# A decoder block on one core: both DRAM writes of a turning ahead of its reads, users six steps on, delayed tasks anchored

## The chip, the cores and the metric

The kernel runs on one core of one Trainium2 chip, as one program. The metric is the device time of one execution in microseconds (us). Engines are PE (matmul), ACT, DVE and POOL (all with queues of their own), and SP, which here only issues DMAs.

## What is computed

One layer of a transformer block on 256 tokens with a width of 2048, in float32. Cut to what matters:

```python
h = h + 0.5 * swiglu(rms_norm(h), ffn1)              # gate, up 2048x5632, down 5632x2048
n = rms_norm(h); P = n @ w_in                        # retention q k v g, window q k v
ret = gate * group_norm(retention(rope(rq), rope(rk), rv))      # 8 heads of 128
swa = sliding_window_attention(rope(sq), rope(sk), sv, sinks)   # 16 heads of 64
h = h + concat(ret, swa) @ w_out
h = h + cross_attention(rms_norm(h), rms_norm(mem))  # 4 heads of 512 into 256 rows
h = h + 0.5 * swiglu(rms_norm(h), ffn2)
out = rms_norm(h)
```

Every one of the products with weights reads its weights from HBM once, 1 MB at a time.

## The kernel before

**Products.** The matrix of each product with weights is cut into units: one unit makes a 256 x 512 piece of an output, `acc`, in two halves of 128 tokens. A step takes 256 rows of the weights (half a MB), so a unit over the depth of 2048 has eight. Weights and activations are each split in a high and a low part of 32 bits, and `three` (L432 to L436) issues high by high (L434), high by low (L435) and low by high (L436). With two slices of 128 rows and two token halves a step is 12 matmuls of 128x128 by 128x512.

**Weights.** `load` and `load_pair` issue 1 MB on SP into `wf` (3 buffers), and `split` makes two steps' parts of it: ACT copies the high part, `wh` (L70), and DVE subtracts for the low part, `wl` (L75). There are 4 buffers of each, and `prepare` splits LOOKAHEAD = 3 steps ahead.

**Turnings.** A result has tokens on its partitions, and its user often needs it the other way round. `cross` (L409) turns two halves of 128x512. DVE transposes blocks of 32x32 (L417) into `sq`, POOL issues a DMA to a DRAM tile `box` (L419, 256 KB) and four DMAs back (L422, 64 KB each) into `dst`, and then the second half goes the same way. POOL issues in order, so the second half's write stands behind the reads of the first, and those wait until the first write has landed. All users of a turning are called by `then`, TURN = 4 steps later. Five functions turn: residual adds (`to_h`, add at L445), the gated FFN blocks (`ffn`, `made`), the retention's q and k (`rqk_done`, `finish` with L690 to L696), the cross attention's keys and queries (`put_done`), and `turn_h`, which brings h back to tokens on partitions in FFN2.

**Behind a residual add** stand the next norm's copies of h (`gained`, L70 on ACT and L329 on DVE), the squares (L362 on ACT), their sum (L366 on DVE) and, two steps after the last, `finish`, whose matmul with ones (L377) gives the mean of squares. The retention scores (`ret_scores`, L705) stand behind `finish` of `rqk_done`. The memory's norm is made in w_out's stage too: `mem_block` loads `mem` on SP (L782) into t2k tiles.

**What sets the order.** `run_stream` writes the steps out in order. Between two steps it runs the tasks that are due: `later(n, f)` sets a task n steps ahead. A scheduler then reorders the instructions of each engine as their dependences and its own times allow; the calls of `pin` fix the order of the first 16 steps as written, and all of SP's. Working tiles come from pools: `t2k` (128x512) has 10 buffers, `blk` 13; `acc` has 2, so a unit's accumulator has to be read by ACT (SILU at L470, scaled copies) or DVE (L477) before the unit two further starts.

**The start** interleaves the first gate and up unit. `prepare` splits one step ahead there.

Of the kernel before, what the change touches and what calls it, by code (L numbers as in the profile page):

```python
# [30 lines left out]
TAIL = 4  # L31
WARM = 9
FIRST = 16
TURN = 4
SWA_EVERY = 5


# [1 line left out]
def decoder_block(ctx: ExitStack, tc: tile.TileContext, a: dict, out: bass.AP):  # L39
# [67 lines left out]
    def when(ready, delay, fn):  # L107
# [5 lines left out]
                later(1, attempt)  # L113
        later(delay, attempt)

    def run_due():
        while True:
            due = [x for x in tasks if x[0] <= clock[0]]
            if not due:
                return  # L120
            x = min(due, key=lambda x: (x[0], x[1]))
            tasks.remove(x)
            x[2]()

    def run_until(ready):
        while not ready():
            x = min(tasks, key=lambda x: (x[0], x[1]))
            tasks.remove(x)
            x[2]()

    class Unit:

# [64 lines left out]
    def pin(engines=None):  # L197

        prev = {}
        for ins in nc.cur_bb.bb.instructions:  # L200
            if engines is not None and ins.engine not in engines:
                continue
            if ins.engine in prev:
                tc.add_manual_dep(
                    ins, prev[ins.engine].name,
                    mybir.DependencyInfo(mybir.DependencyClass.NoSync, mybir.DependencyReason.DATA),
                    reason="program order",
                )
            prev[ins.engine] = ins

    def run_stream():
# [48 lines left out]
        held = []  # L260
        for at, (u, b, ks, _, first, last) in enumerate(steps):
            if at < FIRST:
                prepare(at + 1)
                run_due()
                prepare(at + 2)
            else:
                run_due()
                if at == FIRST:
                    pin()
                prepare(at + 1 + LOOKAHEAD)  # L270
            run_until(lambda: b in u.lhs)
            x = u.lhs[b]
            if first:
                u.acc = [ps_acc.tile([P, 2, 512], F32, tag="acc", name=nm("acc"))] * 2
                if u.per_half:
                    u.acc[1] = ps_acc.tile([P, 2, 512], F32, tag="acc", name=nm("acc"))
            wh, wl = ready.pop(at)
            if at == 0:
                for i, k in enumerate(ks):
                    for t in range(2):  # L280
                        by_tokens(u, u.acc[t], x, wh[:, i : i + 1, :], wl[:, i : i + 1, :], [k], t, first and i == 0, False)
            else:
                for t in range(2):
                    y = (u, u.acc[t], x, wh, wl, ks, t, first, last)
                    if u.per_half and t == 1 and at >= len(steps) - TAIL:
                        held.append(y)
                    else:
                        by_tokens(*y)
            clock[0] += 1
            if last:  # L290
                if u.per_half:
                    u.done(u.acc[0], 0)
                    for y in held:
                        by_tokens(*y)
                    u.done(u.acc[1], 1)
                else:
                    u.done(u.acc[0])
# [106 lines left out]
            nc.vector.tensor_tensor(x, x, r, ALU.mult)  # L404

    def squares_of(x):
        return x.rearrange("p (q g j) -> p q g j", q=4, g=4)

    def cross(src, then, delay=TURN):  # L409

        out = []
        for v in src:
            sq, dst = t2k(), t2k()
            nc.vector.transpose(sq.rearrange("p (g q j) -> p q g j", g=4, q=4), v)  # L417
            box = dram.tile([P, 512], F32, tag="box", name=nm("box"))
            nc.gpsimd.dma_start(box, sq)  # L419
            far = box.rearrange("(i r) (g n) -> g r i n", i=4, g=4)  # L420
            for g in range(4):
                nc.gpsimd.dma_start(dst[32 * g : 32 * g + 32, :].rearrange("p (i n) -> p i n", i=4), far[g])  # L422
            out.append(dst.rearrange("p (i q j) -> p q i j", i=4, q=4))
        later(delay, lambda: then(out))

# [13 lines left out]
    def to_h(w, lhs, factor, blocks, norm=None, then=None):  # L439

        def done(acc, b):
            def add(out):
                for t in range(2):
                    v = hT[b][:, :, t * P : (t + 1) * P].rearrange("p q (a j) -> p q a j", a=4)
                    nc.vector.tensor_tensor(v, v, out[t], ALU.add)  # L445
# [5 lines left out]
            s = [acc[:, t, :] for t in range(2)]  # L451
            if factor != 1.0:
                for t in range(2):
                    s[t] = t2k()
                    copy(s[t], acc[:, t, :], scale=factor)
            cross([squares_of(x) for x in s], add)
        for b in range(4):
            Unit(w, b, 512, lhs, lambda acc, b=b: done(acc, b), blocks, pair=True)

    def ffn(norm, w_gate, w_up, down):  # L460
# [12 lines left out]
        def up_done(b):  # L473
            def done(acc):
# [201 lines left out]
    def rqk_done(g, which):  # L676
        def done(acc):
            def finish(out):
# [21 lines left out]
            cross([squares_of(acc[:, t, :]) for t in range(2)], finish)  # L700
        return done

    def ret_scores(g, i, qk):
# [9 lines left out]
    def rv_done(g):  # L713
        def done(acc):
# [3 lines left out]
            def half(t):  # L718
# [19 lines left out]
                for i in range(4):  # L738
# [70 lines left out]
    def v_done(i):  # L809
# [233 lines left out]
```

## Time and profile before

| what | value |
|---|---|
| median of 3 runs | 2288.42 us (2285.37 to 2296.56) |
| the profiled execution | 2288.49 us |
| its span (first to last instruction) | 2286.7 us |
| PE busy, share of the span | 2203.9 us, 96% |
| DVE, ACT, POOL busy | 1290.5, 1023.8, 309.0 us |
| mean clock granted to PE | 0.982 |
| DMA, mean over the span | 206 GB/s |

A line of a timeline holds start and length of an instruction in us, the engine, the line of the program, the operation with its tiles (buffer numbers left out), and in brackets the engine's idle time ahead of it and the instruction that released it. A released wait ends with the last of its conditions. PEclk is the granted share of PE's full clock.

### The profile page before, as it was taken

How to read it: one execution, taken by the hardware profiler on the slowest of the kernel's cores; microseconds unless marked ns; L12 is line 12 of the kernel's file. 1: busy time of each engine (PE TensorE's matmuls, PEld its weight loads, DVE VectorE, ACT ScalarE, POOL GpSimd, SP SyncE). 2: the span in 40 equal slices, each digit the busy share in tenths (PEclk: the TensorE clock that was granted, in tenths of full speed). 3: DMA queues.
4: the chain of work that ended last, by engine and by line, in shares of the span. 5: the costliest groups of instructions: out<-in, count | busy, mean ns of one | idle time of the engine just before them, and what ended most of it. 6: DMA issues, size and time to landing. Idle time of an engine off the chain costs nothing.

```text
span 2286.7 us, 25822 instructions
## 1 busy us (share of the span) xinstructions
PE 2203.9 (96%) x9868; PEld 1821.7 (80%) x9868; DVE 1290.5 (56%) x1532; ACT 1023.8 (45%) x1257; POOL 309.0 (14%) x557
## 2 busy tenths in 40 slices
PE   9999999999999999989699999999899999999998
PEld 7788888888878888877488878887688888878886
DVE  5655555555556688775455655575455554545554
ACT  5444444444445454544344544454344443444443
POOL 0110111110111101111122001132300100010100
PEclk9999999999999999999799999999899999999999
DMA  6666666666566545545466655476666655566663
GB/s 240 234 208 225 216 225 226 214 215 231 206 224 228 192 167 182 185 148 202 164 212 234 215 187 184 171 251 215 228 205 209 226 198 194 200 205 221 208 221 142
DMA packets 132732, 472.05 MB, mean 206 GB/s; under 512 B 15616, under 2 KB 16384, under 8 KB 132480
## 3 DMA queue, kind: packets, MB, share of 16 engines
q1 hardware_dynamic: 109856, 413.57, 51.7%
q0 software_dynamic: 22464, 56.66, 7.9%
q8 instruction: 77, 1.26, 0.2%
q14 instruction: 47, 0.39, 0.0%
q10 hardware_dynamic: 288, 0.18, 0.0%
HBM read 439.93 MB, written 30.41 MB: 206 GB/s over the span
## 4 chain that ended last, share of the span: by engine, by line
PE 41%; DMA 5%; issue 3%; POOL 2%; ACT 1%; DVE 1%; ACTq 0%; POOLq 0%; DVEq 0%
PE acc L435 13%; PE acc L436 13%; PE acc L434 13%; DMA t2k<-box 3%; DMA box<-t2k 2%; POOL t2k L422 2%; ACT wh L70 1%; DVE wl L75 0%; ACT blk L70 0%; PE tmp L436 0%; PE tmp L377 0%; PE tmp L434 0%; PE tmp L435 0%; DVE t2k L366 0%; ACT t2k L70 0%
## 5 line engine op out<-in xcount | busy, mean ns | idle before, releaser
L75 DVE TENSOR_TENSOR wl<-wf,wh 128x1024 fp32r<-128x1024 f32 (+1 forms) x773 | 938.1, 1221 | 688.1 <-ACT wh L70 687.2
L434 PE MATMUL acc<-wh,blk 128*128 128x512 f32 (+1 forms) x3104 | 1215.4, 392 | 34.4 <-ACT wh L70 22.1
L435 PE MATMUL acc<-wl,blk 128*128 128x512 f32 (+1 forms) x3104 | 1213.8, 391 | 8.9 <-DVE wl L75 8.9
L436 PE MATMUL acc<-wh,blk 128*128 128x512 f32 (+1 forms) x3104 | 1211.9, 390 | 0.0
L70 ACT ACTIVATE wh<-wf 128x1024 fp32r<-128x1024 f32 (+1 forms) x773 | 811.6, 1058 | 888.9 <-PE acc L436 859.4
L434 PEld LDWEIGHTS acc<-wh,blk 128*128 128x128 f32 x3104 | 587.3, 189 | 158.0 <-ACT wh L70 24.7
L435 PEld LDWEIGHTS acc<-wl,blk 128*128 128x128 f32 x3104 | 587.3, 189 | 133.1 <-DVE wl L75 13.6
L436 PEld LDWEIGHTS acc<-wh,blk 128*128 128x128 f32 x3104 | 587.4, 189 | 121.4 <-DVE blk L75 0.4
L422 POOL DMA_DIRECT2D t2k<-box x432 | 235.8, 553 | 397.6 <-DMA box<-t2k 222.3
L419 POOL DMA_DIRECT2D box<-t2k x108 | 61.2, 567 | 1343.7 <-DVE t2k L417 1341.3
L70 ACT ACTIVATE blk<-t2k 128x512 fp32r<-128x512 f32 (+2 forms) x74 | 46.1, 623 | 194.7 <-DMA t2k<-box 192.8
L75 DVE TENSOR_TENSOR blk<-t2k,blk 128x512 fp32r<-128x512 f32 (+1 forms) x66 | 44.7, 678 | 131.7 <-ACT blk L70 131.5
L445 DVE TENSOR_TENSOR h<-h,t2k 128x512 f32<-128x512 f32 x32 | 22.1, 691 | 70.8 <-DMA t2k<-box 70.8
L417 DVE STREAM_TRANSPOSE t2k<-t2k 128x512 f32<-128x512 f32 x76 | 53.6, 705 | 13.4 <-ACT t2k L70 13.4
L70 ACT ACTIVATE blk<-h,gains 128x256 fp32r<-128x256 f32 x64 | 27.6, 498 | 20.5 <-DVE h L445 18.6
L477 DVE SCALAR_TENSOR_TENSOR t2k<-acc,n,t2k 128x512 f32<-128x512 f32 x44 | 31.0, 746 | 7.6 <-PE acc L436 7.6
L470 ACT ACTIVATE t2k<-acc,n 128x512 f32<-128x512 f32 x44 | 27.7, 682 | 16.8 <-PE acc L436 16.7
L70 ACT ACTIVATE blk<-tmp 128x512 fp32r<-128x512 f32 (+2 forms) x49 | 21.5, 450 | 26.3 <-DVE blk L75 12.8
L329 DVE SCALAR_TENSOR_TENSOR blk<-h,gains,blk 128x256 fp32r<-128x256 f32 x64 | 27.0, 480 | 2.4 <-ACT blk L70 2.4
L362 ACT ACTIVATE t2k<-h 128x512 f32<-128x512 f32 x32 | 18.2, 618 | 19.2 <-DVE h L445 19.2
L366 DVE TENSOR_TENSOR t2k<-t2k,t2k 128x512 f32<-128x512 f32 x35 | 23.8, 685 | 3.4 <-ACT t2k L362 1.8
L377 PE MATMUL tmp<-ones,t2k 128*128 128x1 f32 x40 | 6.8, 291 | 15.4 <-DVE t2k L366 15.4
(125 smaller groups left out, 519.4 us busy)
## 6 DMA issues: line engine op xcount, KB each, us to landing
wf<-in_ffn_w_down SPq DMA_DIRECT2D x88, 1024.0 KB, 4.9
wf<-in_ffn_w_gate SPq DMA_DIRECT2D x87, 1024.0 KB, 5.1
wf<-in_ffn_w_up SPq DMA_DIRECT2D x87, 1024.0 KB, 5.4
box<-t2k POOLq DMA_DIRECT2D x108, 256.0 KB, 3.4
t2k<-box POOLq DMA_DIRECT2D x432, 64.0 KB, 3.5
wf<-in_w_in_rqk SPq DMA_DIRECT2D x16, 1024.0 KB, 5.0
wf<-in_w_in_rvg SPq DMA_DIRECT2D x16, 1024.0 KB, 5.1
wf<-in_w_out SPq DMA_DIRECT2D x16, 1024.0 KB, 5.8
```

The lines of the kernel that those rows point to most:

```text
L70: return nc.scalar.activation(dst, src, AF.Copy, **kw)
L75: nc.vector.tensor_tensor(lo, src, hi, ALU.subtract)
L329: nc.vector.scalar_tensor_tensor(x[:, k, 1, :], v[:, k, :], g, x[:, k, 0, :], ALU.mult, ALU.subtract)
L366: nc.vector.tensor_tensor(self.sums, self.sums, y, ALU.add)
L417: nc.vector.transpose(sq.rearrange("p (g q j) -> p q g j", g=4, q=4), v)
L419: nc.gpsimd.dma_start(box, sq)
L422: nc.gpsimd.dma_start(dst[32 * g : 32 * g + 32, :].rearrange("p (i n) -> p i n", i=4), far[g])
L434: nc.tensor.matmul(o, ah, bh, start=start, stop=False)
L435: nc.tensor.matmul(o, ah, bl, start=False, stop=False)
L436: nc.tensor.matmul(o, al, bh, start=False, stop=stop)
L470: nc.scalar.activation(gated[b][t], acc[:, t, :], AF.Silu, scale=norm.scale(t))
L477: nc.vector.scalar_tensor_tensor(s[t], acc[:, t, :], norm.scale(t), s[t], ALU.mult, ALU.mult)
```

## The change

It changes four things.

1. `cross` issues both transposes and both writes first, and then the eight reads. Where the source is a working tile (`room`) the reads land in that tile, and no third tile is taken for a half.
2. TURN is 6 rather than 4. `put_done` asks for 5 steps, and calls `attend` at once instead of one step later. The group norm's halves go from 2 and 3 steps to 4 and 5.
3. `run` executes a delayed task and then ties each of its PE, ACT and DVE instructions behind the last instruction that was written for that engine before the task; the scheduler can't put them ahead of it.
4. At the start, steps 1 to 3 have their weights split in halves, step 1's ahead of two of the norm's copies, and from step 8 the splits run four steps ahead.

```diff
-TURN = 4
+TURN = 6
...
+    def run(x):
+        tasks.remove(x)
+        last = look()
+        at = seen[0]
+        x[2]()
+        for ins in nc.cur_bb.bb.instructions[at:]:
+            if ins.engine in anchored and ins.engine in last:
+                order(last[ins.engine], ins)
...
-                    ready[at] = split(loaded[at], steps[at][0].n, 1)
+                    ready[at] = split(loaded[at], steps[at][0].n, 2 if at < 4 else 1)
...
-                prepare(at + 1)
+                prepare(at + 2 if at == 0 else at + 1)
                 run_due()
-                prepare(at + 2)
+                prepare(at + 2 if at < 8 else at + 1 + LOOKAHEAD)
...
-    def cross(src, then, delay=TURN):
+    def cross(src, then, room=None, delay=TURN):
-        out = []
-        for v in src:
-            sq, dst = t2k(), t2k()
-            nc.vector.transpose(sq.rearrange("p (g q j) -> p q g j", g=4, q=4), v)
+        out, boxes = [], []
+        for i, v in enumerate(src):
+            sq = t2k()
+            nc.vector.transpose(sq.rearrange("p (g q j) -> p q g j", g=4, q=4), squares_of(v))
             box = dram.tile([P, 512], F32, tag="box", name=nm("box"))
             nc.gpsimd.dma_start(box, sq)
-            far = box.rearrange("(i r) (g n) -> g r i n", i=4, g=4)
+            boxes.append(box.rearrange("(i r) (g n) -> g r i n", i=4, g=4))
+        for i, box in enumerate(boxes):
+            dst = t2k() if room is None else room[i]
             for g in range(4):
-                nc.gpsimd.dma_start(dst[...].rearrange("p (i n) -> p i n", i=4), far[g])
+                nc.gpsimd.dma_start(dst[...].rearrange("p (i n) -> p i n", i=4), box[g])
...
-                cross([squares_of(x) for x in s], made)
+                cross(s, made, s)
...
-            later(2, lambda: half(1))
-            later(3, lambda: half(0))
+            later(4, lambda: half(1))
+            later(5, lambda: half(0))
...
                 if then is not None:
-                    later(1, then)
-            cross([squares_of(x) for x in s], made)
+                    then()
+            cross(s, made, s, TURN - 1)
```

Three places in the order of instructions. The first is DVE at the first residual add after FFN1's down product. The names in the rows are of tiles: `wl` low parts of weights, `wf` the loaded weights, `t2k` the turned halves, `h0` the first block of h. Before:

```order
L75 TENSOR_TENSOR wl_766_4612<-wf_764_4609,wh_765_4611 128x1024
L417 STREAM_TRANSPOSE t2k_769_4631<-t2k_767_4627 128x4x4x32
L75 TENSOR_TENSOR wl_776_4650<-wf_764_4609,wh_775_4649 128x1024
L75 TENSOR_TENSOR wl_780_4669<-wf_778_4666,wh_779_4668 128x1024
L417 STREAM_TRANSPOSE t2k_772_4640<-t2k_768_4629 128x4x4x32
L75 TENSOR_TENSOR wl_782_4685<-wf_778_4666,wh_781_4684 128x1024
L445 TENSOR_TENSOR h0_75<-h0_75,t2k_770_4632 128x4x128
L75 TENSOR_TENSOR wl_785_4703<-wf_783_4700,wh_784_4702 128x1024
L75 TENSOR_TENSOR wl_791_4737<-wf_783_4700,wh_790_4736 128x1024
L445 TENSOR_TENSOR h0_75<-h0_75,t2k_773_4641 128x4x128
```

and after (L437 is the transpose, L467 the add):

```order
L75 TENSOR_TENSOR wl_736_4588<-wf_734_4585,wh_735_4587 128x1024
L437 STREAM_TRANSPOSE t2k_739_4607<-t2k_737_4603 128x4x4x32
L437 STREAM_TRANSPOSE t2k_741_4611<-t2k_738_4604 128x4x4x32
L75 TENSOR_TENSOR wl_744_4624<-wf_734_4585,wh_743_4623 128x1024
L75 TENSOR_TENSOR wl_748_4643<-wf_746_4640,wh_747_4642 128x1024
L75 TENSOR_TENSOR wl_750_4659<-wf_746_4640,wh_749_4658 128x1024
L75 TENSOR_TENSOR wl_753_4677<-wf_751_4674,wh_752_4676 128x1024
L75 TENSOR_TENSOR wl_755_4693<-wf_751_4674,wh_754_4692 128x1024
L75 TENSOR_TENSOR wl_758_4711<-wf_756_4708,wh_757_4710 128x1024
L467 TENSOR_TENSOR h0_75<-h0_75,t2k_737_4603 128x4x128
L467 TENSOR_TENSOR h0_75<-h0_75,t2k_738_4604 128x4x128
L75 TENSOR_TENSOR wl_764_4745<-wf_756_4708,wh_763_4744 128x1024
```

The two transposes had two weight splits between them and now stand side by side, and both adds stand together, six weight splits behind the second transpose, where they stood one and three behind it.

The second place is ACT in w_out's stage, from the second of two `wh` of one load. L362 (after: L382) are squares, and `blk` the norms' copies of `mem`. Before:

```order
L70 ACTIVATE wh_1425_8111<-wf_1413_8061 128x1024
L362 ACTIVATE t2k_1423_8106<-t2k_1406_8023 128x512
L362 ACTIVATE t2k_1424_8108<-t2k_1407_8024 128x512
L70 ACTIVATE blk_1438_8184<-t2k_1428_8128,gains_79 128x256 x2
L70 ACTIVATE blk_1438_8184<-t2k_1429_8129,gains_79 128x256 x2
L362 ACTIVATE t2k_1439_8193<-t2k_1428_8128 128x512
L362 ACTIVATE t2k_1440_8196<-t2k_1429_8129 128x512
L362 ACTIVATE t2k_1441_8201<-h1_76 128x512
L362 ACTIVATE t2k_1442_8204<-h1_76 128x512
L70 ACTIVATE wh_1431_8134<-wf_1430_8132 128x1024
L70 ACTIVATE wh_1433_8150<-wf_1430_8132 128x1024
L70 ACTIVATE wh_1436_8168<-wf_1435_8166 128x1024
```

and after:

```order
L70 ACTIVATE wh_1384_8065<-wf_1375_8029 128x1024
L70 ACTIVATE wh_1388_8084<-wf_1387_8082 128x1024
L70 ACTIVATE blk_1390_8100<-t2k_1373_8025,gains_79 128x256 x2
L70 ACTIVATE blk_1390_8100<-t2k_1374_8026,gains_79 128x256 x2
L382 ACTIVATE t2k_1391_8109<-t2k_1373_8025 128x512
L382 ACTIVATE t2k_1392_8111<-t2k_1374_8026 128x512
L70 ACTIVATE wh_1393_8114<-wf_1387_8082 128x1024
L70 ACTIVATE wh_1398_8136<-wf_1397_8134 128x1024
L70 ACTIVATE wh_1400_8152<-wf_1397_8134 128x1024
L70 ACTIVATE wh_1403_8170<-wf_1402_8168 128x1024
L70 ACTIVATE blk_1405_8186<-t2k_1395_8130,gains_79 128x256 x2
```

The squares of h1 stood ahead of `wh_1431`, the next weight split, with the squares and copies of two `mem` tiles; the split (now `wh_1388`) stands ahead of all of these, and h1's squares are five splits further on.

The third place is ACT at the start of FFN2. `L470` (after: L493) is the SILU of the second gate unit, `blk<-t2k` with 128x512 the copies of turned halves of h. Before, from right behind the weight split `wh_2106`:

```order
L70 ACTIVATE blk_2087_11874<-t2k_2068_11777 128x4x128
L70 ACTIVATE wh_2110_11990<-wf_2109_11988 128x1024
L70 ACTIVATE wh_2112_12008<-wf_2109_11988 128x1024
L70 ACTIVATE blk_2033_11619<-t2k_2077_11821 128x512
L70 ACTIVATE wh_2115_12026<-wf_2114_12024 128x1024
L70 ACTIVATE wh_2117_12042<-wf_2114_12024 128x1024
L70 ACTIVATE blk_2034_11620<-t2k_2080_11830 128x512
L70 ACTIVATE wh_2120_12060<-wf_2119_12058 128x1024
L70 ACTIVATE wh_2122_12076<-wf_2119_12058 128x1024
L70 ACTIVATE blk_2033_11619<-t2k_2094_11916 128x512
L70 ACTIVATE wh_2125_12094<-wf_2124_12092 128x1024
L470 ACTIVATE t2k_2104_11967<-acc_2072_11789,n2_109 128x512
```

and after, where `wh_2050` is the split that was `wh_2106`:

```order
L70 ACTIVATE blk_1985_11606<-t2k_2013_11728 128x512
L70 ACTIVATE wh_2050_11919<-wf_2039_11879 128x1024
L493 ACTIVATE t2k_2042_11897<-acc_2016_11737,n2_109 128x512
L493 ACTIVATE t2k_2043_11898<-acc_2016_11737,n2_109 128x512
L70 ACTIVATE wh_2054_11938<-wf_2053_11936 128x1024
L70 ACTIVATE blk_1984_11605<-t2k_2029_11812 128x512
L70 ACTIVATE wh_2056_11956<-wf_2053_11936 128x1024
L70 ACTIVATE blk_1985_11606<-t2k_2030_11817 128x512
L70 ACTIVATE wh_2059_11974<-wf_2058_11972 128x1024
```

The SILU stood seven weight splits behind `wh_2106` and behind a copy of the second turned block of h, `t2k_2094`; now it stands right behind that split and behind the first block's two copies alone. On SP the loads of `dmat` and `mem` stand one weight load later.

More of the change, by code (lines that the diff above doesn't have):

```diff
@@ L114, in when, with order, look @@
         later(delay, attempt)
+    def order(after, ins):
+        tc.add_manual_dep(
+            ins, after.name,
+            mybir.DependencyInfo(mybir.DependencyClass.NoSync, mybir.DependencyReason.DATA),
+            reason="program order",
+        )
+    anchored = (mybir.EngineType.PE, mybir.EngineType.Activation, mybir.EngineType.DVE)
+    seen = [0, {}]
+    def look():
+        known = nc.cur_bb.bb.instructions
+        for ins in known[seen[0] :]:
+            seen[1][ins.engine] = ins
+        seen[0] = len(known)
+        return dict(seen[1])
+    def run(x):
[6 more added lines that the diff above has]
+                order(last[ins.engine], ins)
     def run_due():
@@ L120, in run_due @@
                 return
-            x = min(due, key=lambda x: (x[0], x[1]))
-            tasks.remove(x)
-            x[2]()
+            run(min(due, key=lambda x: (x[0], x[1])))
     def run_until(ready):
         while not ready():
-            x = min(tasks, key=lambda x: (x[0], x[1]))
-            tasks.remove(x)
-            x[2]()
+            run(min(tasks, key=lambda x: (x[0], x[1])))
     class Unit:
@@ L203, in pin @@
             if ins.engine in prev:
[L204 to L208, printed above, removed]
+                order(prev[ins.engine], ins)
             prev[ins.engine] = ins
@@ L406, in squares_of @@
     def squares_of(x):
[L407 to L417 removed]
+        return x if len(x.shape) == 4 else x.rearrange("p (q g j) -> p q g j", q=4, g=4)
+    def cross(src, then, room=None, delay=TURN):
[3 more added lines that the diff above has]
+            nc.vector.transpose(sq.rearrange("p (g q j) -> p q g j", g=4, q=4), squares_of(v))
             box = dram.tile([P, 512], F32, tag="box", name=nm("box"))
             nc.gpsimd.dma_start(box, sq)
[L420 removed]
+            boxes.append(box.rearrange("(i r) (g n) -> g r i n", i=4, g=4))
+        for i, box in enumerate(boxes):
+            dst = t2k() if room is None else room[i]
             for g in range(4):
[L422 removed]
+                nc.gpsimd.dma_start(dst[32 * g : 32 * g + 32, :].rearrange("p (i n) -> p i n", i=4), box[g])
             out.append(dst.rearrange("p (i q j) -> p q i j", i=4, q=4))
@@ L450, in add @@
                     then(b)
-            s = [acc[:, t, :] for t in range(2)]
-            if factor != 1.0:
+            if factor == 1.0:
+                cross([acc[:, t, :] for t in range(2)], add)
+            else:
+                s = [t2k() for _ in range(2)]
                 for t in range(2):
-                    s[t] = t2k()
                     copy(s[t], acc[:, t, :], scale=factor)
-            cross([squares_of(x) for x in s], add)
+                cross(s, add, s)
         for b in range(4):
@@ L699, in finish @@
                         later(1 + i // 2, lambda i=i: ret_scores(g, i, qk))
-            cross([squares_of(acc[:, t, :]) for t in range(2)], finish)
+            cross([acc[:, t, :] for t in range(2)], finish)
         return done
```

## Prediction

> **What bounds the kernel now.** I read the page first, then a table of windows on PE, then the timelines of the engines that PE waits for.
>
> ```profile
> span 2286.7 us, 25822 instructions
> PE 2203.9 (96%) x9868; PEld 1821.7 (80%) x9868; DVE 1290.5 (56%) x1532; ACT 1023.8 (45%) x1257; POOL 309.0 (14%) x557
> ```
>
> PE is busy for 96% of the span, and the next engine, DVE, for 56%. So only two things can be won: the time in which PE stands, and the time in which it runs at a lower granted clock. The windows show where both are (columns: stretch, its length, PE busy with its instructions, granted clock, DMA share, GB/s):
>
> ```profile
> 0.00:60.00 60.00, 53.58 (x222) 0.97 0.65 229
> 100.00:600.00 500.00, 500.00 (x2207) 1.00 0.64 220
> 660.00:690.00 30.00, 24.86 (x102) 0.89 0.53 177
> 755.00:775.00 20.00, 17.11 (x84) 0.91 0.54 191
> 840.00:1000.00 160.00, 149.05 (x717) 0.98 0.48 166
> 1060.00:1145.00 85.00, 58.48 (x231) 0.82 0.48 161
> 1355.00:1380.00 25.00, 21.92 (x114) 0.93 0.48 155
> 1550.00:1570.00 20.00, 16.41 (x64) 0.83 0.49 158
> 1620.00:1645.00 25.00, 13.65 (x52) 0.73 0.58 189
> 2010.00:2025.00 15.00, 13.30 (x51) 0.89 0.60 203
> ```
>
> In steady work (100 to 600 us) nothing is lost: 500/2207 is 0.2266 us for a matmul and 12 of them, one step, take 2.72 us. I price every other window as (length minus busy) plus (1 minus clock) times length. That gives, in order: start 6.42+1.80 = 8.2; 660: 5.14+3.30 = 8.4; 755: 2.89+1.80 = 4.7; 840: 10.95+3.20 = 14.2; 1060: 26.52+15.30 = 41.8; 1355: 3.08+1.75 = 4.8; 1550: 3.59+3.40 = 7.0; 1620: 11.35+6.75 = 18.1; 2010: 1.70+1.65 = 3.4. Together 110.6 us, so the floor is near 2288.5-110.6 = 2178 us. The profiled execution took 2288.49 us, beside a median of 2288.42, so the sum against it holds for the median too.
>
> PE's timeline tells what ended each wait (in brackets the idle time and its releaser):
>
> ```profile
> 679.04 0.79 PE L434 MATMUL acc<-wh,blk 128*128 128x512 f32 x1 [4.68 <-ACT wh L70]
> 764.23 1.08 PE L377 MATMUL tmp<-ones,t2k 128*128 128x1 f32 x8 [2.89 <-DVE t2k L366]
> 989.24 1.19 PE L705 MATMUL tmp<-blk 128*128 128x256 f32 x2 [6.37 <-DVE blk L696]
> 1096.87 0.80 PE L434 MATMUL acc<-wh,blk 128*128 128x512 f32 x1 [13.62 <-ACT wh L70]
> 1131.38 1.87 PE L377 MATMUL tmp<-ones,t2k 128*128 128x1 f32 x8 [8.90 <-DVE t2k L366]
> 1365.83 0.57 PE L434 MATMUL tmp<-blk,blk 128*128 128x256 f32 x1 [3.08 <-ACT blk L70]
> 1557.82 1.86 PE L377 MATMUL tmp<-ones,t2k 128*128 128x1 f32 x8 [3.59 <-DVE t2k L366]
> 1638.01 0.79 PE L434 MATMUL acc<-wh,blk 128*128 128x512 f32 x1 [11.35 <-ACT t2k L470]
> ```
>
> Those of L366, L696 and the `blk` copy are users of a turning or stand right behind one. The waits for `wh` look like a slow weight split, but four splits take 3.88 us of ACT below; they stood in ACT's queue behind such a user. The timelines of POOL, DVE and ACT at the first case show it:
>
> ```profile
> 654.27 0.56 POOL L419 DMA_DIRECT2D box<-t2k  x1 [14.93 <-DVE t2k L417]
> 658.37 2.18 POOL L422 DMA_DIRECT2D t2k<-box  x4 [3.53 <-issue]
> 660.54 0.56 POOL L419 DMA_DIRECT2D box<-t2k  x1
> 667.80 2.18 POOL L422 DMA_DIRECT2D t2k<-box  x4 [6.70 <-DMA box<-t2k]
> ...
> 657.59 0.70 DVE L417 STREAM_TRANSPOSE t2k<-t2k 128x512 f32<-128x512 f32 x1
> ...
> 674.57 0.69 DVE L445 TENSOR_TENSOR h<-h,t2k 128x512 f32<-128x512 f32 x1 [6.83 <-DMA t2k<-box]
> ...
> 675.30 1.70 ACT L70 ACTIVATE blk<-h,gains 128x256 fp32r<-128x256 f32 x4 [10.72 <-DVE h L445]
> ...
> 677.95 3.88 ACT L70 ACTIVATE wh<-wf 128x1024 fp32r<-128x1024 f32 x4
> ```
>
> The second transpose ends at 658.29, but the second write can issue only at 660.54, behind the first half's write and reads on POOL's queue. It lands 7.26 us later, its reads are issued until 669.98, and the add runs at 674.57. From first write to last add: 20.3 us, 7.5 steps, for users that are due four steps (10.9 us) on.
>
> **The change part by part.** *Both writes first.* Nothing is added or removed: the same writes (0.56 us of POOL each) and reads (0.55 each). In this place the two transposes now stand together, so the second write issues about 0.6 us behind the first, at 654.9. Lower bound for its landing: the first write's, 654.27 to 658.37 is 4.10 us, so both are down by 659.0; the eight reads take 4.4 us of POOL from 658.4 and the last is issued at 662.8. Upper bound: it takes the 7.26 us of the old second write, landing at 662.1, with reads until 664.3. The last read to the add was 674.57-669.98 = 4.6 us. So the data is there at 667.4 to 668.9, 13.1 to 14.6 us after the first write. What the second write moves past are the first half's four reads, which start 0.6 us later at most; they release nobody early, as `then` takes both halves.
>
> [...]
>
> *Users six steps on.* Six steps are 16.3 us, and 13.1 to 14.6 fit. The cost is that a user runs 5.4 us later; it is hidden where its result has slack, as in steady FFN work. Where it has none (norm finish, attend), the code moves: the attend call comes at once instead of a step on, and put_done's turnings take five steps.
>
> *Tasks kept behind what was written.* No instruction is added. An early hoist of an ACT user ahead of a weight split can't happen any more, so a late turning no longer stops `wh`. A PE instruction also loses its freedom to be put later. I take zero for the orders themselves and bound it under the rivals.
>
> The big stage is 1060 to 1145:
>
> ```profile
> 1071.41 0.56 POOL L419 DMA_DIRECT2D box<-t2k  x1 [9.31 <-DVE t2k L417]
> ...
> 1076.43 0.56 POOL L419 DMA_DIRECT2D box<-t2k  x1
> 1084.51 2.18 POOL L422 DMA_DIRECT2D t2k<-box  x4 [7.52 <-DMA box<-t2k]
> ...
> 1073.27 0.71 DVE L417 STREAM_TRANSPOSE t2k<-acc 128x512 f32<-128x512 f32 x1
> ...
> 1093.93 0.69 DVE L445 TENSOR_TENSOR h<-h,t2k 128x512 f32<-128x512 f32 x1 [8.11 <-DMA t2k<-box]
> ...
> 1094.72 1.15 ACT L362 ACTIVATE t2k<-h 128x512 f32<-128x512 f32 x2 [9.83 <-DVE h L445]
> 1095.77 3.89 ACT L70 ACTIVATE wh<-wf 128x1024 fp32r<-128x1024 f32 x4
> ...
> 1084.26 1.18 SPq L782 DMA_DIRECT2D t2k<-in_mem  x2
> 1085.49 14.61 SPq L178 DMA_DIRECT2D wf<-in_w_out  x2
> ```
>
> ACT waits 9.83 us for the add of h1, with four weight splits behind it, and PE waits 13.62. In the new order those splits stand ahead of h1's squares. The second write can issue near 1074 (the second transpose of this block ended there) rather than 1076.43. With the old 8.08 us it lands at 1082.1, reads issue until 1084.3, and 7.24 us (1093.93-1086.69) later, at 1091.5, the data is there; with six steps from 1071.4 the users are due at 1087.7. So between 0 and 3.8 us may stay, and then on DVE, since ACT's splits are ahead. SP is the other queue: its `mem` loads wait for free t2k tiles, and a weight load stands behind each pair. They move behind one more weight load, and the t2k tiles come free sooner because reads land in the source tiles. I leave 5.8 us of the 41.8 and take 36 (bounds 20 and 41.8).
>
> At 1620 the SILU of the second gate unit was late in ACT's row:
>
> ```profile
> 1635.23 0.63 ACT L70 ACTIVATE blk<-t2k 128x512 f32<-128x512 f32 x1 [8.29 <-DMA t2k<-box]
> 1635.76 1.04 ACT L70 ACTIVATE wh<-wf 128x1024 fp32r<-128x1024 f32 x1
> 1636.71 1.25 ACT L470 ACTIVATE t2k<-acc,n 128x512 f32<-128x512 f32 x2
> ```
>
> PE needs the accumulator that it frees. It now stands seven weight splits earlier, and ahead of the second `h` turning's copies, of which one (8.29 us of waiting) stood before it: 17 of 18.1 (bounds 9 and 18.1).
>
> The rest: 660, 8 of 8.4 (the working above; bounds 4 and 8.4). 755, 3.5 of 4.7, and 1550, 6 of 7.0: both norm finishes, whose add is earlier by the working above, while PE's place moves little (bounds 0 and all). 840, 9 of 14.2: PE's L705 stands some two steps, 5.4 us, later, against waits up to 6.37; but DVE's mixer work comes in bunches (bounds 0 and 14.2). 1355, 3 of 4.8. 2010, 3 of 3.4. Start: weight step 1 is split in halves and comes ahead of two gained copies; I take half of 8.2, 4; the three splits that are halved cost at most as much again, 3 x 3.88/4 = 2.9 us of ACT, which is busy for 45% of the span and hides it; uncovered, the 4 shrink to 1. Sum: 4+8+3.5+9+36+3+6+17+3 = 89.5, and 2288.5-89.5 = 2199 us.
>
> *What a left-over wait costs.* The waits of 2.89 and 3.08 us each cost 1.8 us of clock besides, as their windows show at 0.91 and 0.93. [...]
>
> **The rivals.** *A, landings stay the limit.* The mid-size stages gain, but writes and reads beside 1 MB loads land as late as 8 us however early they issue. 1060 keeps its second wait, 8.90 us and half its clock loss, 7.65: 16.6 rather than 5.8. 660 and 1620 keep half, 13.3 rather than 1.5. That adds 10.8+11.8: 2199+23 = 2222 us. For it: the 7.5 and 8.1 us waits above. Against: the old chain of 20.3 us is two landings of a write one after the other.
>
> *B, pinned users become new waits.* PE instructions of delayed tasks can't slide behind weight work that is ready, so a user that is 1 us late stops PE and costs 1.7 of clock besides. Four attends, eight value products of the window heads, and two norm finishes, 14 places by 2.7, are 38 us: 2237 us. For it: L705's wait comes from just such a task. Against: tasks have two steps more.
>
> *C, slower.* Turnings hold t2k tiles six steps instead of four in a pool of ten. If SILUs of the 22 gate units then wait for a tile, the accumulator frees late. At a step late, 2.72 plus 1.7 of clock, 22 units cost 97 us and it ends at 2296; from 4.7 us each (22 x 4.7 = 103) it is over 2300. Against: the reads land in their source tiles, so a turning holds four tiles, not six, and 4 x 6 steps equal 6 x 4.
>
> *D, nothing comes of it.* PE's waits are put down to the wrong releaser; the weight loads behind SP's `mem` loads and DVE's bunches set the end of the waits anyway, and what is won at one place is waited for at the next: 2288 us. Against: 674 to 679, where every row up to PE's is a turning.
>
> **How the numbers follow.** Forecast 0.62, with a range of its own from 2180 to 2214; A 0.18; B 0.13; D 0.04; C 0.03. The likeliest gives 2199 us. To hold 8 in 10 the range runs from the floor, about 2180, over A and to B's 2237, with 3 us for the bounds: 2240. What a measurement of this kernel can tell from no change is about 0.5%, 11 us. Forecast, A and B are faster by more: 0.93; D is 0.04; C 0.03.
>
> **What would show it.** In the changed profile POOL's rows have two writes together and then eight reads, from first write to last add 13 to 15 us of data time; PE busy stays at about 2204 minus the matmuls' extra time at half clock; the window of `w_out` has under 8 us of loss, and the SILU of the second gate unit of FFN2 no wait on a copy of `h`. The forecast is wrong if waits over 4 us stand in `w_out` behind `ACT wh` (A), if many short waits of PE on L434 `tmp`, L609 or L377 appear with a clock under 1 (B), or if waits on L470's successor appear in 100 to 600 us (C).

## The result, and the profile after

The changed kernel takes 2206.45 us in the median (2206.03 to 2210.35, 4 runs) against 2289.16 us before (2285.37 to 2296.56, 4 runs): a ratio of 0.9639, with a 95% interval from 0.9612 to 0.9665. 2199 us had been forecast, in a range from 2180 to 2240. Beside the experiments the kernel before was run again several times; its medians there are 2289 to 2295 us.

The page after, first its span, then busy time and clock:

```profile
span 2204.2 us, 25835 instructions
PE 2182.6 (99%) x9868; PEld 1807.8 (82%) x9868; DVE 1291.2 (59%) x1535; ACT 1027.3 (47%) x1260; POOL 309.6 (14%) x557
PEclk9999999999999999999999999999999999999999
```

The span is 82.5 us shorter. PE runs the same 9868 matmuls, and 21.3 us of its busy time are gone too: PE ran for 45.4 us at half clock before and for 6.8 after, and half of the difference, 19 us, is about what half clock had added to its matmuls (in both traces a matmul into an accumulator starts 0.23 us behind the last at full clock, and 0.43 at half). DVE, ACT and POOL do the same work in the same time; only waits went. The windows on PE (stretch, length, PE busy, clock, DMA share, GB/s), moved where the stage now starts earlier:

```profile
0.00:60.00 60.00, 56.74 (x244) 1.00 0.69 248
660.00:690.00 30.00, 30.00 (x134) 1.00 0.79 254
755.00:775.00 20.00, 19.75 (x102) 1.00 0.50 172
840.00:1000.00 160.00, 158.86 (x782) 1.00 0.51 174
1040.00:1125.00 85.00, 79.94 (x351) 0.98 0.73 234
1320.00:1350.00 30.00, 30.00 (x164) 1.00 0.58 195
1560.00:1600.00 40.00, 40.00 (x176) 1.00 0.72 241
1960.00:1990.00 30.00, 30.00 (x134) 1.00 0.72 240
```

Nearly all stages are full. Most of what is left stands in w_out: 5.06 us of waiting and some half clock. The first turning after FFN1's down product now reads like this on POOL and DVE:

```profile
649.04 1.15 POOL L439 DMA_DIRECT2D box<-t2k  x2 [18.96 <-DVE t2k L437]
651.98 4.37 POOL L444 DMA_DIRECT2D t2k<-box  x8 [1.78 <-DMA box<-t2k]
...
663.24 1.51 DVE L467 TENSOR_TENSOR h<-h,t2k 128x512 f32<-128x512 f32 x2
```

Two writes, eight reads, and the first add 14.2 us after the first write, without a wait. In the trace the last read lands 14.9 us after the first write and the second add starts at 15.0, so the six steps just cover the landing here. And the SILU of FFN2's second gate unit, which PE had waited 11.35 us for, now runs in a stretch in which PE never stops (its row on ACT; PE's window 1560 to 1600 above):

```profile
1586.62 1.99 ACT L70 ACTIVATE wh<-wf 128x1024 fp32r<-128x1024 f32 x2
1588.52 1.24 ACT L493 ACTIVATE t2k<-acc,n 128x512 f32<-128x512 f32 x2
```

**Stage by stage.** Both kernels run 9312 matmuls into accumulators in the same order. Subtracting the start times of the n-th one in the two traces gives the time won by each stage, without any pricing. The terms of the forecast stand beside them.

| stage (n-th accumulator matmul) | won, us | forecast |
|---|---|---|
| start, to 240 | 5.2 | 4 |
| FFN1's down product, 2880 to 3120 | 7.4 | 8 |
| mixer norm's finish, to 3360 | 4.1 | 3.5 |
| mixers, to 4320 | 10.7 | 9 |
| w_out, to 5040 | 26.6 | 36 |
| cross attention, 5520 to 6000 | 5.4 | 3 |
| FFN2 norm's finish, to 6480 | 3.2 | 6 |
| FFN2's start, to 6720 | 13.3 | 17 |
| after it | 6.4 | 3 |
| together | 82.1 | 89.5 |

### The profile page after: what moved, and what is told of

Read it like the earlier page. It is cut to its first block, busy times and chain, and to the rows that moved or that the text cites. A ratio compares the mean times of both kernels' runs of the same rounds, so it can differ in the third digit from the quotient of the medians.

```text
span 2204.2 us, 25835 instructions
## 1 busy us (share of the span) xinstructions
PE 2182.6 (99%) x9868; PEld 1807.8 (82%) x9868; DVE 1291.2 (59%) x1535; ACT 1027.3 (47%) x1260; POOL 309.6 (14%) x557
## 4 chain that ended last, share of the span: by engine, by line
PE 88%; issue 5%; DMA 3%; DVE 2%; ACT 1%; POOL 1%; SPq 0%; ACTq 0%; POOLq 0%; DVEq 0%
PE acc L457 28%; PE acc L456 28%; PE acc L458 28%; DMA wf<-in_w_out 1%; DVE wl L75 1%; DMA t2k<-box 1%; DMA wf<-in_ffn_w_up 1%; ACT wh L70 1%; POOL t2k L444 1%; PE tmp L458 0%; PE tmp L457 0%; PE tmp L456 0%; PE tmp L397 0%; PE tmp L632 0%; PE tmp L606 0%
## 5 line engine op out<-in xcount | busy, mean ns | idle before, releaser
L437 DVE STREAM_TRANSPOSE t2k<-t2k 128x512 f32<-128x512 f32 x76 | 49.4, 687 | 19.0 <-ACT t2k L70 19.0
L493 ACT ACTIVATE t2k<-acc,n 128x512 f32<-128x512 f32 x44 | 27.8, 685 | 29.4 <-PE acc L458 29.4
L467 DVE TENSOR_TENSOR h<-h,t2k 128x512 f32<-128x512 f32 x32 | 21.1, 687 | 9.0 <-DMA t2k<-box 8.7
L75 DVE TENSOR_TENSOR blk<-tmp,blk 64x256 fp32r<-64x256 f32 (+2 forms) x41 | 19.2, 474 | 3.0 <-ACT blk L70 2.8
L382 ACT ACTIVATE t2k<-h 128x512 f32<-128x512 f32 x32 | 18.2, 616 | 2.6 <-DVE h L467 2.6
```

The lines of the kernel that those rows point to most:

```text
L75: nc.vector.tensor_tensor(lo, src, hi, ALU.subtract)
L493: nc.scalar.activation(gated[b][t], acc[:, t, :], AF.Silu, scale=norm.scale(t))
```

## The experiments

Three theories were on trial as to the cause: the two landings of a turning in series (theory 1), the place of its users in the queues (theory 2), and the time that t2k tiles are held (theory 3). The runs of one part alone come from one chip, those of one part taken out from another, a_stall and a_memearly from a third, a_both and after_again from a fourth. Medians of the same kernel differ by up to 6 us from chip to chip (the kernel before: 2289.09 to 2295.32). The changed kernel ran beside its variants only as after_again; elsewhere "slower" is against 2206.45. The kernel before took 2289.16 us beside that, and 2289.09 beside the runs of one part taken out.

### One part alone on the kernel before

**b_writes**, both writes first:

```diff
-        out = []
+        out, far = [], []
         for v in src:
-            sq, dst = t2k(), t2k()
+            sq = t2k()
...
+            far.append(box.rearrange("(i r) (g n) -> g r i n", i=4, g=4))
+        for f in far:
+            dst = t2k()
             for g in range(4):
-                nc.gpsimd.dma_start(dst[...], far[g])
+                nc.gpsimd.dma_start(dst[...], f[g])
```

> The kernel before, with only both writes of a turning ahead of its eight reads (reads still land in tiles of their own, users four steps on, nothing anchored). Theory 1, two landings in series are the cause: the data is there after 13 to 15 us rather than 20, which wins most where a chain of turnings stopped the weight splits (660, w_out, FFN2's start): 25 to 45 us, so 2245 to 2265 us. Theory 2, the users' places in the queues are the cause: 4 steps are 10.9 us and the data still comes 2 to 4 us after them, so under 12 us is won.

It took 2242.51 us against 2293.42, a ratio of 0.9764 (0.9710 to 0.9817): 51 us won, more than theory 1 had. The users, due after four steps, still wait. POOL and DVE at the same turning show the data's time directly:

```profile
654.66 1.15 POOL L419 DMA_DIRECT2D box<-t2k  x2 [19.54 <-DVE t2k L417]
658.45 4.36 POOL L424 DMA_DIRECT2D t2k<-box  x8 [2.63 <-DMA box<-t2k]
...
663.64 0.69 DVE L447 TENSOR_TENSOR h<-h,t2k 128x512 f32<-128x512 f32 x1 [2.85 <-DMA t2k<-box]
669.78 0.69 DVE L447 TENSOR_TENSOR h<-h,t2k 128x512 f32<-128x512 f32 x1 [3.18 <-DMA t2k<-box]
```

From the first write to the last add: 15.1 us, where the kernel before took 20.3. Its PE still has the long waits in w_out, shortened:

```profile
1073.57 0.80 PE L436 MATMUL acc<-wh,blk 128*128 128x512 f32 x1 [8.37 <-ACT wh L70]
...
1106.43 1.87 PE L377 MATMUL tmp<-ones,t2k 128*128 128x1 f32 x8 [7.36 <-DVE t2k L366]
```

**b_anchor**, the delayed tasks kept behind what was written:

```diff
+    def run(x):
...
+                order(last[ins.engine], ins)          # as in the change
...
-            x = min(due, key=lambda x: (x[0], x[1]))
-            tasks.remove(x)
-            x[2]()
+            run(min(due, key=lambda x: (x[0], x[1])))
...
```

> The kernel before, with only the delayed tasks' instructions kept behind what was written ahead of them. Theory 2, users hoisted ahead of weight splits stop ACT: 30 us or more are won (under 2260 us). Theory 1, landings in series: the users are still due 9 us before their data, so they wait at the head of the queue as before, and it stays within 10 us of 2289, or gets slower.

2270.99 us, a ratio of 0.9888 (0.9831 to 0.9946): 22 us won, between the two expectations. The windows of w_out and of FFN2's start show what the anchors do alone:

```profile
1060.00:1145.00 85.00, 72.58 (x305) 0.96 0.64 216
1520.00:1545.00 25.00, 17.31 (x77) 0.91 0.62 200
1600.00:1640.00 40.00, 26.47 (x106) 0.87 0.60 188
```

In w_out, 26.5 us of waiting have become 12.4 with data as late as before (at h1's turning POOL has issued the last read 15.0 us after the first write, 15.3 before): weight splits no longer stand behind a user that waits. The norm's finish (second row) and FFN2's start (third) are as slow as before or slower.

**b_turn6**, the users six steps on:

```diff
-TURN = 4
+TURN = 6
...
-            later(2, lambda: half(1))
-            later(3, lambda: half(0))
+            later(4, lambda: half(1))
+            later(5, lambda: half(0))
...
-                    later(1, then)
-            cross([squares_of(x) for x in s], made)
+                    then()
+            cross([squares_of(x) for x in s], made, TURN - 1)
```

> The kernel before, with only the users six steps on (keys' and queries' turnings five and attend at once; group norm halves at 4 and 5). Theory 1: 16.3 us against a chain of 20.3 us leave 4 us of wait where there were 9, about half the gain, 2240 to 2260 us. Theory 2, the scheduler hoists users however late they are called: within 10 us of 2289. Theory 3, six steps hold the ten t2k tiles, three per half, too long: slower than 2289, with waits for accumulators in the steady FFN stretches.

2257.38 us, a ratio of 0.9837 (0.9779 to 0.9894): 36 us won, as theory 1 had it. FFN1's steady stretch loses nothing, although turnings here hold three tiles a half for six steps, so theory 3 falls there: from 100 to 600 us PE is busy for all 500.

**b_first**, the other order of the first 16 steps:

```diff
-                    ready[at] = split(loaded[at], steps[at][0].n, 1)
+                    ready[at] = split(loaded[at], steps[at][0].n, 2 if at < 4 else 1)
...
-                prepare(at + 1)
+                prepare(at + 2 if at == 0 else at + 1)
                 run_due()
-                prepare(at + 2)
+                prepare(at + 2 if at < 8 else at + 1 + LOOKAHEAD)
```

> The kernel before, with only the other order of the first 16 steps. All theories: only the first 60 us change. The same matmuls were reached 5.2 us sooner in the changed kernel, so 2284 us, and nothing else moves; if the start hangs together with the rest, it differs from that by over 3 us.

2288.61 us against 2293.42, a ratio of 0.9970 (0.9947 to 0.9992). That fits the 5 us of the start; the interval would hold 2 us or 12 as well.

The four win 51, 22, 36 and 5 us, 114 together, where all of them at once win 83. So the first three replace each other in part.

### One part taken out of the changed kernel

**a_turn4**, the users four steps on:

```diff
-TURN = 6
+TURN = 4
...
-            later(4, lambda: half(1))
-            later(5, lambda: half(0))
+            later(2, lambda: half(1))
+            later(3, lambda: half(0))
...
-                    then()
-            cross(s, made, s, TURN - 1)
+                    later(1, then)
+            cross(s, made, s)
```

> The changed kernel with users four steps on again (attend one step after its turning, group norm halves at 2 and 3). Theory 1, 13 to 15 us of data time against 10.9: waits of 2 to 4 us plus clock at some ten places without slack, 30 to 50 us slower than 2206. Theory 2, the anchors alone hold the weight splits ahead: under 12 us slower.

2226.14 us: 20 us slower, between the two. Most of it are the norm finishes, which come when the data isn't there (PE's timeline, twice; then DVE's at the second):

```profile
1124.14 1.07 PE L397 MATMUL tmp<-ones,t2k 128*128 128x1 f32 x8 [4.15 <-DVE t2k L386]
...
1509.67 1.87 PE L397 MATMUL tmp<-ones,t2k 128*128 128x1 f32 x8 [8.00 <-DVE t2k L386]
...
1504.04 1.46 DVE L467 TENSOR_TENSOR h<-h,t2k 128x512 f32<-128x512 f32 x2 [8.33 <-DMA t2k<-box]
```

**a_oldcross**, the old order of a turning:

```diff
...
-            boxes.append(box.rearrange("(i r) (g n) -> g r i n", i=4, g=4))
-        for i, box in enumerate(boxes):
+            box = box.rearrange("(i r) (g n) -> g r i n", i=4, g=4)
             dst = t2k() if room is None else room[i]
```

> The changed kernel with the old order of a turning: write, four reads, write, four reads (reads land in the source tiles still). Theory 1: the chain of 20 us exceeds 16.3 by 4, which costs 20 to 40 us at the places without slack. Theory 2: the six steps and the anchors cover it, under 10 us slower.

2215.44 us: 9 us slower. But the edit changed less than its text says. POOL's order is left to the scheduler, and in 37 of the 54 turnings it still put both writes ahead of the reads; POOL's rows at the first turning after FFN1's down product and, behind them, at one in w_out:

```profile
650.09 1.15 POOL L439 DMA_DIRECT2D box<-t2k  x2 [18.98 <-DVE t2k L437]
653.01 4.36 POOL L443 DMA_DIRECT2D t2k<-box  x8 [1.77 <-DMA box<-t2k]
...
1045.51 0.56 POOL L439 DMA_DIRECT2D box<-t2k  x1 [7.64 <-DVE t2k L437]
1048.51 2.17 POOL L443 DMA_DIRECT2D t2k<-box  x4 [2.44 <-issue]
1050.67 0.56 POOL L439 DMA_DIRECT2D box<-t2k  x1
1058.38 2.17 POOL L443 DMA_DIRECT2D t2k<-box  x4 [7.15 <-DMA box<-t2k]
```

The old order came back in 17: the first turning, the retention's q and k, the four of w_out, the cross attention's residual adds and four at FFN2's start. There six steps and the anchors cover most of the longer chain. What the order is worth in the other 37 beside the other parts, no run shows. One place is left over:

```profile
1502.83 1.87 PE L397 MATMUL tmp<-ones,t2k 128*128 128x1 f32 x8 [5.12 <-DVE t2k L386]
```

**a_free**, without the anchors:

```diff
-        for ins in nc.cur_bb.bb.instructions[at:]:
-            if ins.engine in anchored and ins.engine in last:
-                order(last[ins.engine], ins)
```

> The changed kernel without the anchors: the scheduler may put delayed tasks ahead of what was written before them. Theory 2, hoisted users stop ACT and DVE: 20 us or more slower than 2206, with waits of PE for wh and wl. Theory 1, once the data is in time the place matters little: within 10 us.

2218.60 us: 12 us slower, again between the two. In w_out, where about half of it is lost, PE waits longer for splits:

```profile
1063.42 0.80 PE L453 MATMUL acc<-wh,blk 128*128 128x512 f32 x1 [3.40 <-ACT wh L70]
...
1091.45 0.50 PE L453 MATMUL acc<-wh,blk 128*128 128x512 f32 x1 [2.49 <-ACT wh L70]
```

**a_noroom**, reads into tiles of their own:

```diff
-            dst = t2k() if room is None else room[i]
+            dst = t2k()
```

> The changed kernel with the reads of every turning in a t2k tile of their own. Theory 3, t2k tiles held for six steps are short: SILUs and the mem loads wait for a tile, and it is 20 us or more slower, mostly in w_out and at FFN2's start. Otherwise within 8 us.

2208.97 us (2205.32 to 2209.80), not told apart from 2206.45: tiles for the reads are no bound here.

### What a wait costs

**a_stall** adds three waits to the changed kernel in FFN1:

```diff
+            if at in STALLS:                        # {58: 1, 90: 3, 122: 6}
+                ts = tmp_ps()
+                for q4 in range(4):
+                    nc.tensor.matmul(ts[:, q4 * P : (q4 + 1) * P], ident, ident, start=True, stop=True)
+                jk = t2k()
+                copy(jk, ts)
+                for _ in range(STALLS[at]):
+                    nc.gpsimd.tensor_tensor(jk, jk, jk, ALU.mult)
+                ts2 = tmp_ps()
+                nc.tensor.matmul(ts2[:, :P], ident, jk[:, :P], start=True, stop=True)
+                halt = look()[mybir.EngineType.PE]
...
+                        order(halt, ins)        # the step's first matmul stands behind it
...
```

> The changed kernel with three waits put into FFN1's steady stretch, at steps 58, 90 and 122: a 128x512 product with ident (four matmuls), an ACT copy, then 1, 3 and 6 POOL multiplications in a row, and a matmul on their result that the next weight matmul stands behind. Added work only. It measures what a wait of PE costs. Theory A (the prediction's pricing): wait plus half of the time shown at half clock. Theory B: wait plus half of only that part of it in which PE was running; half clock while PE stands costs nothing. For waits of 2 to 4 us both give about the wait plus 1.7; for a wait over 7 us A gives 3.4 or more on top, B no more than 1.7.

It took 2231.55 us in its one run, 25 us more. PE's rows at the three, and the windows around them:

```profile
171.62 0.49 PE L310 MATMUL tmp<-t2k,ident 128*128 128x128 f32 x2 [2.41 <-POOL t2k L308]
264.73 0.79 PE L310 MATMUL tmp<-t2k,ident 128*128 128x128 f32 x2 [4.64 <-POOL t2k L308]
364.87 0.79 PE L310 MATMUL tmp<-t2k,ident 128*128 128x128 f32 x2 [9.31 <-POOL t2k L308]
```

```profile
166.00:174.00 8.00, 5.59 (x30) 1.00 0.67 212
258.00:274.00 16.00, 11.36 (x45) 0.79 0.39 131
354.00:372.00 18.00, 8.69 (x35) 0.72 0.46 143
```

Against the changed kernel's accumulator matmuls the three cost 3.82, 8.44 and 12.58 us. At the first the clock stayed full, so 3.82-2.41 = 1.41 us are the added matmuls. That leaves 8.44-4.64-1.41 = 2.4 us for the second's clock and 12.58-9.31-1.41 = 1.9 for the third's. By theory A the windows would give (1-0.79) x 16 = 3.4 and (1-0.72) x 18 = 5.0. By theory B only the part counts in which PE ran: the half clock lasted to 269.8 and 368.8, PE ran again from 264.73 and 364.87, and half of 5.1 and 3.9 is 2.5 and 2.0. Theory B holds for both; the expectation's limit of 1.7 for it was too tight by 0.2 at the third wait.

### A better version

**a_memearly** calls the mem loads six steps earlier:

```diff
+    def mem_early(b):                # called when the unit's accumulator is done
         if b == 0:
             for b in range(4):
                 later(1 + 4 * b, lambda b=b: mem_block(b))
...
-    to_h(a["w_out"], mixT, 1.0, (2, 3, 0, 1), None, out_done)
+    to_h(a["w_out"], mixT, 1.0, (2, 3, 0, 1), None, out_done, mem_early)
```

> The changed kernel with the four mem loads and their norm called when the first w_out unit ends, not when its residual add is made six steps later. In the changed kernel ACT's weight splits waited for w_out's weight loads, up to 7.4 us, which stood behind mem loads on SP. If SP's order is what is left in w_out, the waits of 1.1 and 2.4 us there go and with them their clock, some 5 us: 2201 us. If the mem loads wait for t2k tiles wherever they stand, the weight loads stand behind them earlier and it is the same or up to 10 us slower.

2206.55 us, no difference; against the kernel before on its own chip the ratio is 0.9621, beside 0.9639. w_out is 1 us shorter up to its end: one wait of 3.43 us replaced two of 1.13 and 2.40, and the second expectation is the one that held.

**a_both** adds to this the squares ahead of the gained copies:

```diff
-                    norm.block(b, [hT[b]])
-                    norm.stat([hT[b]])
+                    norm.stat([hT[b]])
+                    norm.block(b, [hT[b]])
```

> The changed kernel with the mem loads called early as in a_memearly, and with a residual add's squares and their sum ahead of the next norm's gained copies of h. Work is only reordered. If the wait at n2's finish, 1.6 to 2.9 us plus 1.7 to 3.4 at half clock, is set by the 1.7 us of gained copies ahead of the sum on ACT and DVE, it goes, 2 to 5 us less: 2201 to 2204 us. If the landing of the reads sets it, or the copies then come late for the next products, it stays within 2 us of 2206.

> The changed kernel once more, unchanged, so that the version a_both stands beside it on one chip: 2206 us, within 4.

2202.97 us (2201.75 to 2206.71) beside 2208.80 (2207.37 to 2209.79) for **after_again** on the same chip: 5.8 us faster, without overlap, and the fastest version here (0.9605 of before, 0.9587 to 0.9623). Between the two traces 5.9 us are won around FFN2's norm; the squares' order alone was not run. PE's row at FFN2's norm, first after_again, then a_both:

```profile
1497.42 1.87 PE L397 MATMUL tmp<-ones,t2k 128*128 128x1 f32 x8 [3.22 <-DVE t2k L386]
```

```profile
1493.45 1.05 PE L397 MATMUL tmp<-ones,t2k 128*128 128x1 f32 x8 [0.56 <-DVE t2k L386]
```

What is left in a_both is w_out. Its SP and ACT there:

```profile
1022.74 5.72 SPq L202 DMA_DIRECT2D wf<-in_w_out  x2
1045.63 1.23 SPq L808 DMA_DIRECT2D t2k<-in_mem  x2
1046.96 0.89 SPq L202 DMA_DIRECT2D wf<-in_w_out  x2
...
1056.80 2.00 ACT L70 ACTIVATE wh<-wf 128x1024 fp32r<-128x1024 f32 x2 [11.78 <-DMA wf<-in_w_out]
```

After 1028.46 SP issues nothing until 1045.63, where the second pair of mem loads goes out, and the weight load behind it comes 1.3 us later; ACT waits for it. The profile puts 17.0 us of SP's wait down to the landing of a turning's write (`box<-t2k`, issued at 1043.17), which reads a t2k tile: by it, the mem pair waits for a tile that a turning gives back, and a_memearly has the same 17.0 us. No run takes that wait away, so what it costs stays open.

## Why the prediction was right, and where it was off

- *What bounds the kernel.* Right. PE's waits were what could be won, and other engines' busy time didn't change.
- *Both writes first.* The mechanism was right. The data's time was put at 13.1 to 14.6 us; b_writes shows 15.1 at that turning, since its last reads, issued by 662.81, are used at 669.78, 7.0 us on, where 4.6 was taken from the old order. Over all 54 turnings the median from the first write's issue to the last read's landing is 16.2 us before, 13.6 in b_writes and 13.6 after; the 20.3 of the forecast's case was one of the longest. At this turning the second write had landed 5.4 us after the first was issued in b_writes and 3.3 in the changed kernel, where the forecast has 4.7 to 7.8; it is the reads that came late. The 16.3 us of six steps do not count from the first write, as the forecast has it: ACT's copies and the first transpose come ahead of it, and the first add stood 14.2 us behind it. With the last read landing at 14.9 the fit was close, and not 1.7 to 3.2 us of slack.
- *Tasks kept behind what was written.* The forecast took zero for the orders themselves. Alone they win 22 us, and the changed kernel loses 12 without them. The reason given, a late user ahead of a weight split, was right for w_out.
- *Held tiles.* Rival C's mechanism didn't show: neither b_turn6 nor a_noroom stops PE in the steady stretch from 100 to 600 us.
- *The step that failed is the price of a window*, "(length minus busy) plus (1 minus clock) times length". It counts half clock while PE stands as a loss, on top of the standing. In the trace of before, 78.5 us at half clock lie ahead of the last matmul, and PE ran in only 45.4 of them. With waits of 72.6 us the loss was 72.6+45.4/2 = 95.3, not 110.6. So the floor was near 2288.5-95.3 = 2193 us and not 2178, and the range's lower end of 2180 lay under what the end of every wait could give. The profile carries the same test 13 times: the end of the last matmul less waits less half the running time at half clock lies from 2178.2 to 2184.2 us for before, after, after_again and ten experiments (all but a_stall). With all time at half clock it goes from 2166.0 (before) to 2181.6.
- *The terms that this mis-sized.* w_out: of 30.7 us at half clock PE ran in 13.1, so 41.8 should have been 33.1; 26.6 were won. FFN2's start: 18.1 should have been 11.35+4.3/2 = 13.5, and 13.3 were won, all of it. The forecast of 89.5 was 7.4 too high, and these two are 13.1 too high and FFN2's norm 2.8. Some 9 us of that were made up by stages that won more than was forecast for them (the start, the mixers, the cross attention, the end); nothing in the forecast says why they should, so that part of the closeness to 2199 is luck.
- *What was left over.* w_out kept 5.06 us of waits and a clock loss of 1.7, 6.8 against the 5.8 left to it. Of rival A this much is true: ACT waited there for weight loads (its row in the changed kernel), so SP and the DMAs are what is late next. Its sign, waits of PE over 4 us behind `wh`, did not show: the longest is 2.40 (first PE's row, then SP's and ACT's).

```profile
1085.97 0.49 PE L456 MATMUL acc<-wh,blk 128*128 128x512 f32 x1 [2.40 <-ACT wh L70]
...
1074.42 0.38 SPq L202 DMA_DIRECT2D wf<-in_w_out  x1
...
1084.86 2.00 ACT L70 ACTIVATE wh<-wf 128x1024 fp32r<-128x1024 f32 x2 [7.44 <-DMA wf<-in_w_out]
```

- FFN2's norm finish, for which 6 of 7.0 were taken, gave 3.2: the finish stayed pinned two steps behind its last add, and a wait of 1.63 us stayed, with 3.4 us at half clock behind it. a_both shows that the gained copies ahead of the sum were part of it.
- *Rival B* did not come: the pinned users in the mixers and the cross attention stop PE for 0.2 to 1.1 us each, without half clock (1.00 from 840 to 1000 us, and from 1309 to 1313 behind the wait of 1.11), where 1.7 of clock had been put to each.
- *The clock.* For each of the waits of 2.89 and 3.08 us the prediction took 1.8 us of clock from the windows, and behind both the trace has PE busy at a clock of 0.50 (765.2 to 768.5 us and 1365.9 to 1369.2). The length of one wait alone doesn't decide here: in a_stall a wait of 2.41 us left the clock full (1.00 from 166 to 174 us), and one of 1.63 us at FFN2's norm in the changed kernel stood 2 us ahead of 3.4 us at half clock (0.50 from 1498 to 1501.4). PE's row there:

```profile
1496.12 1.05 PE L397 MATMUL tmp<-ones,t2k 128*128 128x1 f32 x8 [1.63 <-DVE t2k L386]
```

## What to carry to other kernels

When several edits all shorten one chain or loosen its due date, test each alone and each taken away: here they won 114 us one by one, 83 together, and cost 9 to 20 where they were taken out. See in the trace that an edit did what it was to do: a_oldcross restored the old order in 17 turnings of 54. Price half clock only where the engine runs; a stretch at half clock under a wait was paid for by the wait here (a_stall: 2.4 and 1.9 us of clock, where the whole windows would give 3.4 and 5.0). Where an engine prepares weights for PE, look for users of slow transfers ahead of the next piece in its queue: both an earlier transfer and an order that is written down shortened such waits here (PE's longest wait behind `wh` in w_out was 13.62 us before and 8.37 in b_writes, and all its waiting there 26.5 us before and 12.4 in b_anchor).

## What the runs showed of the hardware

With both writes first and eight reads in a row, the reads land later and the writes sooner. The reads of 64 KB take 3.5 us from issue to landing before, 4.9 after, and the writes of 256 KB 3.4 and 2.9. In b_writes, where nothing else was changed, they take 5.1 and 2.9. The page's rows after:

```profile
box<-t2k POOLq DMA_DIRECT2D x108, 256.0 KB, 2.9
t2k<-box POOLq DMA_DIRECT2D x432, 64.0 KB, 4.9
```

So a part of what the second write wins is given back by the reads. In b_turn6, with the old order throughout, they take 3.6; in a_oldcross, with the old order in 17 turnings of 54, 4.4.
